# FFN-in: the lo parts of the weight operands and of the next pass's left operands computed on VectorE

## The chip, the cores and the metric

The kernel runs on one core of a Trainium2 chip. The metric is the device time of one execution in microseconds (us). Five engines work side by side, each through its own queue in order: TensorE (PE; its weight loads are PEld), VectorE (DVE), ScalarE (ACT), GpSimd (POOL), and SyncE (SP), which here only issues DMAs.

## The reference

One layer of a decoder over a prompt of 2048 tokens and 8 sample tokens, width 1024: norm, an input projection into a convolution group and a differential-attention group, an output projection, and a SwiGLU FFN of inner width 2816, all in float32. The change lies in the first half of the FFN:

```
h2 = rmsnorm(x, g_ffn) * (1 + sc_f) + sh_f
gg, uu = jnp.split(h2 @ w_ffn_in, 2, axis=-1)
x = x + gt_f * ((jax.nn.silu(gg) * uu) @ w_ffn_out)
```

## The kernel before

**Precision.** A float32 product is made of three TensorE products. Each operand is split into hi, a rounded copy (fp32r) that ScalarE casts, and lo, the operand minus hi, made by a subtraction on an engine that the caller names; then lo x hi, hi x lo and hi x hi are accumulated. The split is `split_sb` (lines 187 to 189): line 188 is the cast, line 189 the subtraction. Every lo part in the program carries line 189, so they are told apart by their tiles.

**FFN-in** (`phase_ffn_in`, lines 1097 to 1249) multiplies 2048 prompt rows and the 8 sample rows by w_ffn_in in three passes of 2 x 344 columns of h2 transposed (HW = 344, NPASS = 3). In a pass the product is a 2 x 2 block product done with seven block products instead of eight. The left operands of a pass are seven combinations a11, s1, s3, s2, a12, s4, a22 of the transposed rows, 128 x 1376 each, split into hi and lo tiles `cha..`/`cla..` and `chs..`/`cls..`; there is one buffer of each. A pass has 22 tiles of the inner width (f and f + 11 form a pair), 66 in all. `tile_f` (line 1149) does one tile:

- `w_combos` (line 1118) loads the two weight blocks of the tile (`wr`, four buffers), forms four block differences t1, t3, t2, t4 on VectorE (line 1128, tiles `tr`, four buffers), and splits the seven right operands b11, t1, t3, t2, b21, b22, t4, 128 x 512 each, into `wh`/`wl` tiles, one buffer for each operand. So an operand of the next tile can be split as soon as its block product of this tile is done, and must be there a tile later. Before, t1 and t4 have their lo part on VectorE and the other five on GpSimd (lines 1136 to 1146).
- seven block products of 12 matmuls each (line 1161), into PSUM tiles `in` (six buffers, four a tile);
- ScalarE copies one result (line 1167) and applies silu (lines 1175, 1180); VectorE adds the others from PSUM (line 1164, five a tile) and multiplies by silu (line 1181).

After each pair, `pair` (line 1184) makes the gating sums that the next phase's block product needs, four operations of 128 x 344 on GpSimd (lines 1193 to 1196), and SyncE stores them to gD (line 1200). The loads of the weight blocks (line 123, `ld`) go through the same SyncE queue.

During a pass, `next_raws` (line 1202) prepares the next pass: it loads rows, transposes them on TensorE (line 899, eight at a time), and forms the sums s1, s3, s2, s4 (line 907; s2 on GpSimd, the others on VectorE). At the end of the pass (lines 1245 to 1247) the seven new left operands are split; before, those with i % 3 == 2, s3 and s4, on GpSimd, the others on VectorE. The left operands of pass 0 are made by `first_combos` and by lines 1113 to 1116, which the change leaves as they are: a22 has its lo part on GpSimd there.

**Order.** Nothing in the kernel fixes the order across tiles. The program is traced in the order of the code, and the framework (`schedule_with_timeline_sim=True`, line 1534) lays out each engine's queue at build, by the dependences, the buffers and a simulated timeline. So an operation of the next tile stands between those of this one where the timeline found room. On the chip every queue runs in the order laid out.

Of the kernel before, what the change touches and what calls it, by code (L numbers as in the profile page):

```python
# [82 lines left out]
class Kern:  # L83
# [1013 lines left out]
    def phase_ffn_in(self, raws, comb):  # L1097
# [12 lines left out]
        dv, gp = nc.vector, nc.gpsimd  # L1110
        split = lambda *x: self.block_split(wp, *x)
# [6 lines left out]
        def w_combos(f):  # L1118

            raw = []  # L1120
            for part in range(2):
                r = self.t(wp, [P, KD, P], F32, "wr", bufs=4)
                c0 = part * DFF + f * P
                self.ld(r, I["w_ffn_in"][0, :, c0:c0 + P].rearrange("(k p) n -> p k n", p=P))
                raw.append(r.rearrange("p k n -> p (k n)"))
            b11, b21, b12, b22 = (raw[i][:, 512 * q:512 * (q + 1)] for i in range(2) for q in range(2))
            t1, t3, t2, t4 = (self.t(wp, [P, 512], F32, "tr", bufs=4) for _ in range(4))
            sub = lambda o, x, y: dv.tensor_tensor(out=o, in0=x, in1=y, op=ALU.subtract)
            out = {}

            def wsplit(i, name, r, eng):
                hi, lo = (self.t(wp, [P, 512], F32R, f"w{x}{i}") for x in "hl")
                self.split_sb(hi, lo, r, eng)
                out[name] = tuple(t.rearrange("p (k n) -> p k n", k=4) for t in (hi, lo))

            wsplit(0, "b11", b11, gp)
            sub(t1, b12, b11)
            wsplit(1, "t1", t1, dv)
            sub(t3, b22, b12)
            wsplit(2, "t3", t3, gp)  # L1140
            sub(t2, b22, t1)
            wsplit(3, "t2", t2, gp)
            wsplit(4, "b21", b21, gp)
            wsplit(5, "b22", b22, gp)
            sub(t4, b21, t2)
            wsplit(6, "t4", t4, dv)
            return out

        def tile_f(f, p, g):


            w = w_combos(f)
            t = self.t(wp, [P, 3, HW], F32, "nat", bufs=2)
            s, u2, u4 = (t[:, i] for i in range(3))
# [29 lines left out]
        def pair(f, p, work):  # L1184

            x = self.t(wp, [P, 3, HW], F32, "xt", bufs=3)
            y = self.t(wp, [P, 3, HW], F32, "xt", bufs=3)
            tile_f(f, p, x)
            work()
            t = tile_f(f + NF // 2, p, y)  # L1190
            work()
            cs = slice(HW * p, HW * (p + 1))
            gp.tensor_tensor(out=x[:, 2], in0=x[:, 1], in1=y[:, 1], op=ALU.add)
            gp.tensor_tensor(out=y[:, 2], in0=x[:, 2], in1=x[:, 0], op=ALU.subtract)
            gp.tensor_tensor(out=x[:, 1], in0=x[:, 0], in1=x[:, 1], op=ALU.subtract)
            gp.tensor_tensor(out=t[:, 0], in0=y[:, 0], in1=y[:, 2], op=ALU.subtract)

            st = nc.scalar if (f, p) == (NF // 2 - 1, NPASS - 1) else nc.sync
            for i, src in ((0, x), (3, y), (6, t[:, 0:1])):
                st.dma_start(out=self.gD[f][:, i:i + src.shape[1], cs], in_=src)  # L1200

        def next_raws(p):

            raws = self.new_raws()
            lo, w = half_pos(p)
            hi = lo + 2 * w

            pst = lambda: self.t(self.ps, [P, 512], F32, "tp", bufs=2)
            if w < HW:
                ht = self.t(wp, [DEC, D], F32, "gt")  # L1210
                self.ld(ht, self.h2sD)
                for q in range(2):
                    dv.memset(raws[1, q][:, :, w:], 0.0)
                    pt = pst().rearrange("p (k t) -> p k t", k=4)
                    for k in range(4):
                        nc.tensor.transpose(pt[:, k, 0:DEC], ht[:, (4 * q + k) * P:(4 * q + k + 1) * P], self.ident[:DEC, :DEC])
                    nc.scalar.copy(out=raws[0, q][:, :, w:], in_=pt[:, :, 0:DEC])
            for tt in range(lo // P, -(-hi // P)):
                self.turn_x1(raws, p, tt, "gt" if tt % 2 else "A2", pst)
                yield  # L1220
            s1, s2, s4 = (self.t(wp, [P, 4, HW], F32, f"rw{x}") for x in ("s1", "s2", "s4"))
            self.block_sum(s1, raws[1, 0], raws[1, 1], ALU.add, dv)
            yield
            self.block_sum(raws[1, 0], raws[0, 0], raws[1, 0], ALU.subtract, dv)
            self.block_sum(s2, s1, raws[0, 0], ALU.subtract, gp)
            yield
            self.block_sum(s4, raws[0, 1], s2, ALU.subtract, dv)
            yield {"a11": raws[0, 0], "s1": s1, "s3": raws[1, 0], "s2": s2, "a12": raws[0, 1], "s4": s4, "a22": raws[1, 1]}

        for p in range(NPASS):  # L1230
            ahead = next_raws(p + 1) if p + 1 < NPASS else iter(())
            nxt, done = None, 0

            def work():
                nonlocal nxt, done
                done += 1
                if (p, done) == (0, 4):
                    self.roots(6, 11)
                    self.roots(11, NT)
                if done > 6:  # L1240
                    nxt = next(ahead, nxt)

            for f in range(NF // 2):
                pair(f, p, work)
            if nxt:
                for i, (name, raw) in enumerate(nxt.items()):
                    comb[name] = split(name, raw, gp if i % 3 == 2 else dv)
        self.close("l3")
        self.close("r4")

# [287 lines left out]
```

## Time and profile before

| | |
|---|---|
| runs shown | median 2721.44 us of 3 (2715.95 to 2722.97) |
| profiled execution | 2719.35 us, its span 2717.6 us |
| TensorE clock granted, mean | 0.978 |
| HBM read and written | 283.10 MB, 106.12 MB |
| HBM traffic | 143 GB/s over the span |

Times are us from the start of the span, durations of one instruction ns where marked so. "Busy" counts the time from an instruction's start to its end, also when it is held up inside. "<-" behind a wait names what ended it. In the FFN-in stage the first matmul starts at 1297.0 and the last ends at 2234.7. The stretches used below begin and end where a tile's 84 matmuls do: at the starts of every 84th matmul of line 1161.

### The profile page before, as it was taken

How to read it: one execution, taken by the hardware profiler on the slowest of the kernel's cores; microseconds unless marked ns; L12 is line 12 of the kernel's file. 1: busy time of each engine (PE TensorE's matmuls, PEld its weight loads, DVE VectorE, ACT ScalarE, POOL GpSimd, SP SyncE). 2: the span in 40 equal slices, each digit the busy share in tenths (PEclk: the TensorE clock that was granted, in tenths of full speed). 3: DMA queues.
4: the chain of work that ended last, by engine and by line, in shares of the span. 5: the costliest groups of instructions: out<-in, count | busy, mean ns of one | idle time of the engine just before them, and what ended most of it. 6: DMA issues, size and time to landing. Idle time of an engine off the chain costs nothing.

```text
span 2717.6 us, 38141 instructions
## 1 busy us (share of the span) xinstructions
PE 2563.3 (94%) x13470; PEld 2154.6 (79%) x13470; DVE 1913.7 (70%) x2905; ACT 1250.5 (46%) x2385; POOL 1268.9 (47%) x902
## 2 busy tenths in 40 slices
PE   8999999998799998999799999999999989999997
PEld 3466767776687866777799999999899987778875
DVE  3269889987997887776767777776867653455467
ACT  4434222127797875473445343544434434333333
POOL 0100134024632223332667777667877753465573
PEclk9999999998999998999899999999999999999998
DMA  8635224238433314343344434434344435767555
GB/s 275 210 114 195 94 105 140 98 144 246 147 97 114 94 44 146 120 142 106 104 130 130 133 107 133 152 105 134 99 133 123 132 119 185 254 209 228 158 175 183
DMA packets 343991, 391.24 MB, mean 144 GB/s; under 512 B 31828, under 2 KB 258271, under 8 KB 343793
## 3 DMA queue, kind: packets, MB, share of 16 engines
q1 hardware_dynamic: 335945, 370.80, 42.6%
q10 hardware_dynamic: 7856, 18.01, 1.9%
q8 instruction: 106, 1.74, 0.3%
q14 instruction: 84, 0.69, 0.1%
HBM read 283.10 MB, written 106.12 MB: 143 GB/s over the span
## 4 chain that ended last, share of the span: by engine, by line
PE 51%; DVE 10%; issue 8%; POOL 5%; DMA 2%; ACT 2%; SPq 0%; ACTq 0%; POOLq 0%; DVEq 0%
PE in L1161 26%; PE o L1341 8%; PE one L155 2%; PE one L156 2%; PE one L154 2%; DVE p L660 2%; POOL wl L189 1%; PE two L655 1%; PE two L656 1%; PE x L844 1%; POOL w L1273 1%; POOL z L1273 1%; PE x L154 1%; DVE p L675 1%; PE x L156 1%
## 5 line engine op out<-in xcount | busy, mean ns | idle before, releaser
L1341 PE MATMUL o<-b,a 128*128 128x512 f32 x1848 | 431.8, 395 | 13.9 <-POOL b L189 11.4
L1341 PEld LDWEIGHTS o<-b,a 128*128 128x128 f32 x1848 | 348.0, 188 | 97.1 <-POOL b L189 12.2
L1161 PE MATMUL in<-cls,wh 128*128 128x344 f32 x1056 | 335.6, 324 | 27.3 <-DVE nat L1164 10.3
L1161 PE MATMUL in<-chs,wl 128*128 128x344 f32 x1056 | 341.5, 323 | 8.0 <-DVE wl L189 8.0
L189 POOL TENSOR_TENSOR wl<-wr,wh 128x512 fp32r<-128x512 f32 x198 | 296.2, 1504 | 107.3 <-ACT wh L188 105.9
L1161 PE MATMUL in<-chs,wh 128*128 128x344 f32 x1056 | 339.3, 321 | 0.0
L477 DVE SCALAR_TENSOR_TENSOR y<-u,cw,y 128x1024 f32<-128x1024 f32 x240 | 307.8, 1305 | 2.1
L188 ACT CAST wh<-tr 128x512 fp32r<-128x512 f32 x264 | 162.7, 620 | 207.0 <-PE in L1161 180.9
L1161 PE MATMUL in<-cla,wh 128*128 128x344 f32 x792 | 256.5, 324 | 1.2 <-ACT wh L188 0.7
L1161 PE MATMUL in<-cha,wl 128*128 128x344 f32 x792 | 254.9, 322 | 0.0
L1161 PE MATMUL in<-cha,wh 128*128 128x344 f32 x792 | 252.5, 321 | 0.0
L189 POOL TENSOR_TENSOR wl<-tr,wh 128x512 fp32r<-128x512 f32 x132 | 200.3, 1521 | 86.0 <-ACT wh L188 82.2
L672 POOL TENSOR_TENSOR p<-p,p 128x384 f32<-128x384 f32 (+9 forms) x60 | 109.0, 1819 | 251.6 <-ACT p L671 204.2
L498 POOL TENSOR_TENSOR ropet<-ev,tab 128x128 f32<-128x128 f32 x32 | 21.4, 670 | 433.5 <-ACT ev L531 433.1
L1161 PEld LDWEIGHTS in<-cls,wh 128*128 128x128 f32 x1056 | 199.0, 190 | 30.8 <-DVE nat L1164 10.8
L1161 PEld LDWEIGHTS in<-chs,wl 128*128 128x128 f32 x1056 | 200.6, 190 | 9.1 <-DVE wl L189 9.1
L1161 PEld LDWEIGHTS in<-chs,wh 128*128 128x128 f32 x1056 | 201.0, 190 | 0.0
L189 POOL TENSOR_TENSOR b<-wr,b 128x512 fp32r<-128x512 f32 x77 | 125.6, 1648 | 155.1 <-ACT b L188 155.0
L189 DVE TENSOR_TENSOR a<-gr,a 128x1032 fp32r<-128x1032 f32 (+1 forms) x77 | 116.6, 1522 | 109.1 <-ACT a L188 109.0
L188 ACT CAST wh<-wr 128x512 fp32r<-128x512 f32 x198 | 122.5, 620 | 100.2 <-POOL wl L189 46.0
L664 ACT ACTIVATE p<-p,st 128x384 f32<-128x384 f32 (+15 forms) x128 | 156.4, 1224 | 20.2 <-DVE st L660 15.3
L154 PE MATMUL one<-w,hTh 128*128 128x512 f32 x384 | 154.4, 405 | 8.0 <-DVE w L189 4.8
(351 smaller groups left out, 6487.4 us busy)
## 6 DMA issues: line engine op xcount, KB each, us to landing
wr<-in_w_ffn_in SPq DMA_DIRECT2D x132, 512.0 KB
gD<-xt SPq DMA_DIRECT2D x64, 516.0 KB
wr<-in_w_ffn_out SPq DMA_DIRECT2D x99, 256.0 KB
gr<-gD SPq DMA_DIRECT2D x44, 516.0 KB
w<-in_w_in SPq DMA_DIRECT2D x80, 256.0 KB
gr<-gD SPq DMA_DIRECT2D x33, 512.0 KB
xt<-in_x_prompt SPq DMA_DIRECT2D x32, 512.0 KB
a<-in_w_ada SPq DMA_DIRECT2D x64, 256.0 KB
```

Source lines behind the costliest of these rows:

```text
L154: mm(ps, lhsT=wh, rhs=xl, start=start, stop=False)
L155: mm(ps, lhsT=wl, rhs=xh, start=False, stop=False)
L156: mm(ps, lhsT=wh, rhs=xh, start=False, stop=stop)
L188: self.nc.scalar.copy(out=hi, in_=raw)
L189: (eng or self.nc.gpsimd).tensor_tensor(out=lo, in0=raw, in1=hi.bitcast(F32), op=ALU.subtract)
L477: nc.vector.scalar_tensor_tensor(out=y, in0=u[:, j:j + HALF], scalar=self.cw[:, ct, j:j + 1], in1=y, op0=ALU.mult, op1=ALU.add)
L660: dv.tensor_tensor_reduce(out=pc[:, lo:hi], in0=sc[:, 0:w], in1=add, scale=1.0, scalar=m, op0=ALU.add, op1=ALU.min, accum_out=mo)
L664: nc.scalar.activation(pc[:, 0:L], pc[:, 0:L], AF.Exp, bias=m, scale=-1.0, accum_out=l)
L672: nc.gpsimd.tensor_tensor(out=a, in0=a, in1=b, op=ALU.add)
L1161: nc.tensor.matmul(ps, lhsT=wt[:, k, :], rhs=xt[:, k, :], start=not more and k == 0 and j == 0, stop=k == 3 and j == 2, skip_group_check=True)
L1273: op = lambda e, o, x, y, k: e.tensor_tensor(out=o, in0=x, in1=y, op=k)
L1341: mm = lambda x, y, s, e: nc.tensor.matmul(ps[i], lhsT=a[:, x, sl], rhs=b[:, y], start=s, stop=e, skip_group_check=True)
```

## The change

Two edits in `phase_ffn_in`. The five lo parts of a tile that were on GpSimd (b11, t3, t2, b21, b22) are on VectorE, so that all seven are; and the lo parts of all seven left operands of the next pass are on VectorE. The casts, the products, the additions, the gating sums and the buffers are as before.

```diff
-            wsplit(0, "b11", b11, gp)
+            wsplit(0, "b11", b11, dv)
             sub(t1, b12, b11)
             wsplit(1, "t1", t1, dv)
             sub(t3, b22, b12)
-            wsplit(2, "t3", t3, gp)
+            wsplit(2, "t3", t3, dv)
             sub(t2, b22, t1)
-            wsplit(3, "t2", t2, gp)
-            wsplit(4, "b21", b21, gp)
-            wsplit(5, "b22", b22, gp)
+            wsplit(3, "t2", t2, dv)
+            wsplit(4, "b21", b21, dv)
+            wsplit(5, "b22", b22, dv)
             sub(t4, b21, t2)
             wsplit(6, "t4", t4, dv)
...
             if nxt:
-                for i, (name, raw) in enumerate(nxt.items()):
-                    comb[name] = split(name, raw, gp if i % 3 == 2 else dv)
+                for name, raw in nxt.items():
+                    comb[name] = split(name, raw, dv)
```

## Rows read from the trace of the kernel before

**Rows 1.** The page, busy time, share of the span and instructions.
```profile
PE 2563.3 (94%) x13470; PEld 2154.6 (79%) x13470; DVE 1913.7 (70%) x2905; ACT 1250.5 (46%) x2385; POOL 1268.9 (47%) x902
```
**Rows 2.** Stretch, length, busy PE, PEld, DVE, ACT, POOL (instructions); clock, DMA share, GB/s.
```profile
1297.00:1329.35 32.35, 18.51 (x92) 17.75 (x93) 28.50 (x35) 15.10 (x28) 22.98 (x12) 0.74 0.27 82
...
1479.85:1510.87 31.02, 27.38 (x170) 26.40 (x169) 29.51 (x27) 12.63 (x23) 26.79 (x16) 1.00 0.36 112
1510.87:1603.51 92.64, 92.64 (x591) 92.64 (x590) 62.70 (x85) 38.09 (x70) 66.87 (x49) 1.00 0.41 128
1603.51:1651.75 48.24, 42.51 (x254) 41.16 (x253) 45.32 (x43) 23.09 (x38) 41.52 (x23) 0.96 0.32 98
...
1748.62:1828.04 79.42, 73.85 (x446) 72.98 (x445) 61.34 (x64) 39.92 (x86) 53.42 (x36) 0.94 0.35 110
...
1920.68:1968.78 48.10, 42.53 (x254) 41.17 (x253) 45.66 (x41) 23.19 (x38) 42.14 (x23) 0.96 0.33 99
```
**Rows 3.** The chain, 1400 to 1430: start, length, what; one set of transposes.
```profile
1418.35 0.88 PE tp L899 x8
```
**Rows 4.** Timeline of VectorE in ordinary tiles: start, duration, operation.
```profile
2107.05 1.42 DVE L189 TENSOR_TENSOR wl<-tr,wh 128x512 fp32r<-128x512 f32 x1
2109.14 1.03 DVE L1128 TENSOR_TENSOR tr<-wr,wr 128x512 f32<-128x512 f32 x1 [0.67 <-DMA wr<-in_w_ffn_in]
...
2119.21 0.86 DVE L1181 TENSOR_TENSOR xt<-xt,dm 128x688 f32<-128x688 f32 x1
2119.99 0.68 DVE L1128 TENSOR_TENSOR tr<-wr,tr 128x512 f32<-128x512 f32 x1
2120.60 0.68 DVE L189 TENSOR_TENSOR wl<-tr,wh 128x512 fp32r<-128x512 f32 x1
```
**Rows 5.** Timeline of GpSimd, the same tiles.
```profile
2106.61 1.31 POOL L1193 TENSOR_TENSOR xt<-xt,xt 128x344 f32<-128x344 f32 x1 [2.12 <-DVE xt L1181]
2107.89 1.74 POOL L189 TENSOR_TENSOR wl<-tr,wh 128x512 fp32r<-128x512 f32 x1
```
**Rows 6.** Groups of VectorE in the stage: count, busy us, mean ns, idle before.
```profile
L1164 DVE TENSOR_TENSOR xt<-in,nat 128x344 f32<-128x344 f32 x132 | 68.0, 515 | 70.0 <-PE in L1161 67.9
```
**Rows 7.** Line 189, whole span: count, duration ns min/median/max, first and last start.
```profile
L189 POOL TENSOR_TENSOR wl<-wr,wh x198: 1275/1301/2661, 1305.1 to 2223.5; 128x512 fp32r<-128x512 f32 x198
...
L189 DVE TENSOR_TENSOR wl<-tr,wh x132: 676/925/3653, 1314.6 to 2224.7; 128x512 fp32r<-128x512 f32 x132
...
L189 DVE TENSOR_TENSOR cls<-rws,chs x4: 1580/1906/2235, 1611.0 to 1935.2; 128x1376 fp32r<-128x1376 f32 x4
L189 POOL TENSOR_TENSOR cls<-rws,chs x3: 3614/3616/4248, 1209.5 to 1941.2; 128x1376 fp32r<-128x1376 f32 x3
```
**Rows 8.** Line 1196 in the stage, one of the four gating sums.
```profile
L1196 POOL TENSOR_TENSOR nat<-xt x32: 914/932/1385, 1354.9 to 2219.5; 128x344 f32<-128x344 f32 x32
```
**Rows 9.** Waits of SyncE's queue in the stage: us in total, times, longest.
```profile
SPq L123 <- POOL wl L189: 434.8, 126, 10.5
```
**Rows 10.** Waits of VectorE in the stage.
```profile
DVE xt L1164 <- PE in L1161: 67.9, 52, 4.7
DVE tr L1128 <- DMA wr<-in_w_ffn_in: 46.0, 37, 2.5
DVE B L1164 <- PE in L1161: 42.7, 31, 1.4
DVE dm L1164 <- PE in L1161: 32.3, 25, 1.4
```
**Rows 11.** Timeline of VectorE at the entry.
```profile
1302.12 3.58 DVE L1128 TENSOR_TENSOR tr<-wr,wr 128x512 f32<-128x512 f32 x1
...
1314.62 0.68 DVE L189 TENSOR_TENSOR wl<-tr,wh 128x512 fp32r<-128x512 f32 x1
```
**Rows 12.** Timeline of GpSimd at the entry.
```profile
1300.71 4.44 POOL L189 TENSOR_TENSOR cla<-rw,cha 128x1376 fp32r<-128x1376 f32 x1
```

## The prediction

> **What bounds the kernel now.** I began with the busy shares of the page [rows 1]: over the whole span VectorE (DVE) is at 70% and GpSimd (POOL) at 47%, so by shares there is room on GpSimd and less on VectorE, and the change moves work the wrong way. An average over stages says little, so next I cut the FFN-in stage at the starts of tiles and took busy time by stretch [rows 2]. A tile here is one call of tile_f, 84 matmuls; there are 66. The stretch from 1510.87 to 1603.51 holds seven tiles and TensorE is busy for all of its 92.64 us, so a tile costs 92.64 / 7 = 13.23 us when nothing is late. There TensorE is the only bound, and a faster VectorE or GpSimd gains nothing. What can be won or lost is in the other stretches, each against 13.23 us a tile:
> - the entry, one tile in 32.35: 19.1 us lost;
> - the block sums of the pass that follows, two tiles in 31.02: 4.6 us lost;
> - the change from pass 0 to pass 1, three tiles in 48.24: 8.5 us lost;
> - the transposes and block sums late in pass 1: five tiles in 79.42, which is 13.3 over; four sets of eight transposes at 0.88 us each [rows 3] are TensorE's own work, so 9.7 us lost;
> - the change from pass 1 to pass 2, three tiles in 48.10: 8.4 us lost.
>
> That is 50 us, 1.8% of the time, and no part of the change reaches another stage. The next view says why those stretches are late. In the order of time on VectorE [rows 4] a 512-column subtraction takes 0.68 us and the next one starts 0.61 us later, but others take 1.42 and 1.03. Beside them stand GpSimd's rows [rows 5]: its instruction from 2106.61 ends at 2107.92, and the VectorE subtraction begun at 2107.05 ends at 2108.47, 0.55 us after that. GpSimd's next, from 2107.89 to 2109.63, takes 1.74 us instead of some 1.26, and the VectorE subtraction begun at 2109.14 ends 0.54 us after it. So an operation of GpSimd and one of VectorE with both inputs in SBUF do not overlap here: the later one waits, and the recorded duration holds the wait. The two engines are one resource for such work. Operations that read one input from PSUM don't show this: their mean is 0.52 us [rows 6].
>
> **That resource, per tile.** The shortest durations stand for work without a wait [rows 7]: 1.27 us for a 512-column lo part on GpSimd; 0.68 on VectorE, of which 0.61 counts in a row. Before: on VectorE six 512-column operations (2 lo parts, 4 block differences) at 0.61 and one product at 0.78 (2119.21 to 2119.99, [rows 4]), 4.4 us; on GpSimd five lo parts at 1.27 and two gating sums (four per pair of tiles) at 0.91 [rows 8], 8.2 us. Together 12.6 of 13.23 us, 95% taken. In an ordinary tile that just fits; where anything is added, it doesn't, and TensorE waits.
>
> **The change, part by part.**
> 1. Five lo parts a tile leave GpSimd (330 in all): 5 x 1.27 = 6.4 us a tile given back. On VectorE they come as 5 x 0.61 = 3.1 us. The resource falls to 12.6 - 6.4 + 3.1 = 9.3 us, 70%.
> 2. VectorE's own queue: eleven operations at 0.61, five additions from PSUM at about 0.5, the product at 0.78: 10.0 us a tile. To that come waits for the gating sums that stay on GpSimd, between none and all of them, 0 to 1.8 us: 10.0 to 11.8 of 13.23. Before, it is busy 62.70 / 7 = 8.96 us a tile [rows 2], of which 7.0 is its own work by the same prices (six operations, five additions, the product) and 2.0 is waiting for GpSimd. So the ordinary tile costs nothing: its 3.1 us more lie beside TensorE's 13.23. If that cover went, every 0.1 us a tile would cost 66 x 0.1 = 6.6 us.
> 3. At each of the two pass changes the lo parts of s3 and s4 (1376 columns) move too: two times 3.61 us off GpSimd, two times 1.58 onto VectorE [rows 7].
> 4. The waits that move. The next tiles' weight loads in SP's queue wait for the last reader of a raw block, until now a GpSimd lo part for 126 of them [rows 9], and the stores of the gating results stand in the same queue. Now VectorE releases the blocks; a lo part there takes half as long but stands behind additions that wait for TensorE. VectorE already waits 46.0 us in 37 places for these loads [rows 10], with lo parts queued behind. An earlier release saves at most those 46 us of slack, and a later one adds to them; a lo part is needed about six products (six sevenths of 13.23, some 11 us) after its slot comes free, so I take 0 for both and keep the effect for the slower rival. ScalarE's casts into the same slots then wait for VectorE instead of GpSimd; same reason, 0.
>
> **The sum, by stretch.** The loss is less than the excess over TensorE's time, because slots give some slack: in the first pass change the resource needed 3 x 12.6 + 5 x 1.58 + 2 x 3.61 = 52.9 us for tiles of 39.7 in all, an excess of 13.2 for a loss of 8.5, so about 4.7 us is forgiven.
> - Pass changes: afterwards VectorE's queue is the longer of the two: 3 x (10.0 to 11.8) + 7 x 1.58 = 41.1 to 46.5 us, an excess of 1.4 to 6.8; less 4.7, a loss of 0 to 2.1. Since an in-order queue also waits, I take 3.5 left of 8.5: 5 us saved at each, ends 0 and 8.5.
> - Block sums of pass 0: the resource needed 2 x 12.6 + 3 x 1.58 + 3.61 (the sum s2 on GpSimd, by the lo part of its shape) = 33.6 for 26.5; VectorE afterwards 2 x 10.0 + 4.7 plus up to 3.6 of waiting for s2 and up to 3.6 for the gating sums: 24.7 to 32. Saved 0 to 4.6, taken 2.
> - Pass 1's late stretch has the same sums and besides transposes fed by loads: saved 0 to 6, taken 2.
> - The entry: the first difference of weight blocks takes 3.58 us instead of 0.68, behind a GpSimd split of 4.44 us that the change leaves there [rows 12], and t1's lo part comes only at 1314.62 [rows 11]. The lo parts that leave GpSimd free a few waits of about 1 us, and come into the same VectorE queue ahead of t1. Ends 3 lost and 8 saved, taken 2.
>
> Saved: 5 + 5 + 2 + 2 + 2 = 16 us. The profiled execution took 2719.35 us (span 2717.6), so 2703 against it; it lies 2 us under the median of the runs, 2721.44, and I give the median's side: 2705.
>
> **Against a rule.** VectorE's busy time in the ordinary stretch is 62.70 of 92.64 us, 68% [rows 2]. The Trainium skill, Perfetto Trace Analysis, section Identifying the Most-Contended Engine, takes the occupancy of VectorE as a fair measure of how near it is to its limit, and its section on Optimizing Scalar/DVE Operations would hand work from a saturated VectorE to other engines, GpSimd included. By that, 8.96 + 3.1 = 12.0 us a tile, 91%, and any stretch with more work saturates; the rows speak against it, since 2.0 of the 8.96 is waiting that goes.
>
> **The rivals.**
> A. *No change that can be measured.* A measurement of this kernel tells about 0.3%, 8 us, from nothing. The order of each engine's instructions is laid down at build from estimated times, and in it VectorE's heads wait for TensorE and for loads; then the stretches are late for that order, not for GpSimd. Saved 1 to 2 us at each pass change and nothing else: about 2718. For it: the first wait of the entry isn't touched. Against: the excess of 13.2 us at a pass change is mostly GpSimd's durations.
> B. *VectorE's in-order queue becomes the bound of the ordinary tile.* Its additions already wait for TensorE 67.9 + 42.7 + 32.3 = 142.9 us in the stage [rows 10], 2.2 a tile. If those waits stay where they are and the gating sums are waited for in full, 11.8 + 2.2 = 14.0 us is over 13.23. It decides once both waits together pass 3.2 us a tile. Halfway, at 0.4 us over on 60 tiles, 24 us are lost, less some 10 recovered: 2721 + 14 = 2735; at the full 0.8, near 2757. This is the case that the rule above describes. Against: a queue that is late finds TensorE's results ready, so such waits shrink first.
> C. *The change does more.* All of the loss at the pass changes and most at the sums goes: 8.5 + 8.4 + 4.6 + 6 + 4 = 31 us, 2690. This is the far end of the forecast, not a case of its own sign.
>
> **How the numbers follow.** Forecast (faster by 8 us or more, C included) 0.60, A 0.26, B 0.14. The likeliest time is 2705; its own range runs from 2690 to 2713. To leave out no more than 2 in 10 the range must hold A with the spread of the runs, to 2723, and the near end of B: 2690 to 2728.
>
> **What would show it.** Right: in the ordinary stretches of seven tiles still 92.6 us with GpSimd's busy time down from 66.87 to some 13 to 19 us and VectorE's up from 62.70 to between 70 and 83; VectorE's 512-column lo parts close to 0.68 us at the median; three tiles of a pass change in 43 to 44 us. Wrong: ordinary tiles longer than 13.3 us with TensorE waiting for VectorE's lo parts (B); pass changes still near 48 us with VectorE idle in them (A); an entry longer than 35 us; or VectorE operations still near 1 us while GpSimd is idle, which would mean that the wait wasn't GpSimd's.

## The result, and the profile after

The changed kernel takes 2683.11 us (median of 4 runs, 2680.43 to 2686.02) against 2721.03 us for the kernel before: a ratio of 0.9856, interval 0.984 to 0.9872. It is faster by 38 us; 2705 was predicted, with 2690 as the lower end of the range. The profiled execution took 2683.30 us, its span is 2681.5. Ratios, here and below, are of fast runs; two slow executions, 14162.85 us of the kernel before and 9932.47 us of the last kernel below, are not in them.

The first part of the page, busy time over the whole span, to hold beside [rows 1]:

```profile
PE 2553.9 (95%) x13470; PEld 2148.5 (80%) x13470; DVE 2000.0 (75%) x3239; ACT 1257.0 (47%) x2385; POOL 763.7 (28%) x568
```

VectorE has 334 instructions more and GpSimd 334 fewer. GpSimd gave up 505 us of busy time, and VectorE took on only 86 us for the same work. 330 lo parts at 0.61 us alone are 201 us, so over 100 us of what VectorE had recorded as busy before was waiting.

The next rows are stretches of the stage in the changed kernel, cut at the starts of the same tiles as in [rows 2] (stretch, length, busy PE, PEld, DVE, ACT, POOL with instructions; clock, DMA share, GB/s): the entry, the block sums of pass 0, seven ordinary tiles, the first pass change, the late stretch of pass 1, the second pass change.

```profile
1299.14:1324.14 25.00, 16.70 (x97) 16.39 (x98) 24.96 (x40) 15.80 (x32) 7.96 (x2) 0.80 0.41 127
1473.75:1500.61 26.86, 26.76 (x169) 26.43 (x169) 25.79 (x34) 11.73 (x21) 9.41 (x5) 1.00 0.40 124
1500.61:1593.31 92.70, 92.70 (x591) 92.70 (x589) 80.07 (x121) 38.99 (x70) 20.30 (x16) 1.00 0.43 133
1593.31:1636.14 42.83, 42.83 (x278) 42.11 (x277) 41.96 (x62) 30.53 (x58) 5.28 (x4) 1.00 0.46 141
...
1729.93:1799.13 69.20, 69.20 (x446) 68.72 (x445) 59.27 (x86) 38.89 (x85) 15.25 (x9) 1.00 0.40 121
...
1891.85:1932.01 40.16, 39.96 (x255) 39.70 (x253) 40.16 (x56) 22.22 (x35) 5.86 (x4) 1.00 0.38 110
```

In all but the entry PE's busy time fills the length to within 0.2 us: TensorE is now the bound there, as it was before in the ordinary tiles alone. VectorE has little left in the second pass change: it is busy for all of the 40.16 us. Row by row against [rows 2]:

| stretch | before | after | difference | predicted |
|---|---|---|---|---|
| entry, 1 tile | 32.35 | 25.00 | -7.35 | -2 |
| block sums of pass 0, 2 tiles | 31.02 | 26.86 | -4.2 | -2 |
| ordinary, 7 tiles | 92.64 | 92.70 | 0 | 0 |
| first pass change, 3 tiles, and the 7 after it | 145.11 | 136.62 | -8.5 | -5 |
| late in pass 1, 5 tiles | 79.42 | 69.20 | -10.2 | -2 |
| second pass change, 3 tiles | 48.10 | 40.16 | -7.9 | -5 |
| the other 38 tiles | 508.96 | 507.32 | -1.6 | 0 |

The first pass change stands with the seven tiles behind it, since 24 transposes moved from those into it (278 instructions on PE instead of 254). The stage as a whole goes from 937.7 to 897.8 us. It starts 2.1 us later and what follows it takes 1.7 us longer, which leaves the 36.1 us by which the span is shorter. Over TensorE's pace of 13.23 us a tile, and some 0.11 us for each of the stage's 104 transposes, it lost some 52.6 us before and 12.7 after, and 10.4 of those 12.7 are in the entry.

Not all of the gain is waiting that went away. These are the sums over the stage's stretches (length, busy time of each engine), before and after:

```profile
sum 937.60, PE 901.86 PEld 895.14 DVE 682.10 ACT 416.03 POOL 677.69; mean PE 90.19 PEld 89.51 DVE 68.21 ACT 41.60 POOL 67.77
```

```profile
sum 897.86, PE 889.24 PEld 886.48 DVE 766.33 ACT 422.42 POOL 174.55; mean PE 88.92 PEld 88.65 DVE 76.63 ACT 42.24 POOL 17.46
```

TensorE stands still for 35.7 us before (937.60 - 901.86) and for 8.6 after, 27.1 us less. The other 12.6 us are time in which it works, though its instructions are the same. Most of that, some 10 us, is its clock. In the rows of the two pass changes and of the late stretch of pass 1 it was granted at 0.96, 0.96 and 0.94 before [rows 2], and at 1.00 after; (1 - clock) x length is 8.6 us there, and outside the entry TensorE's busy time fell by 10.8. At the entry the clock was 0.74 and is 0.80, a difference of some 2 us of work. The first pass change before shows it (TensorE, start and duration):

```profile
1636.91 0.40 PE L1161 MATMUL in<-cls,wh 128*128 128x344 f32 x1 [4.03 <-POOL xt L1193]
...
1638.00 0.49 PE L1161 MATMUL in<-chs,wh 128*128 128x344 f32 x1
1638.29 0.49 PE L1161 MATMUL in<-cls,wh 128*128 128x344 f32 x1
```

TensorE had stood still for 4.03 us, and soon after it its matmuls start 0.29 us apart, at the lower level of its clock (1.2 GHz), instead of 13.23 / 84 = 0.16. So a wait costs its own length and slower work behind it, and the prediction has no term for the second.

VectorE's waits in the stage (us in total, times, longest), to hold beside [rows 10]:

```profile
DVE tr L1128 <- DMA wr<-in_w_ffn_in: 46.8, 41, 3.3
...
DVE xt L1164 <- PE in L1161: 19.1, 15, 2.8
DVE B L1164 <- PE in L1161: 11.0, 19, 1.4
DVE dm L1164 <- PE in L1161: 9.9, 20, 0.6
```

The additions wait 40.0 us for TensorE, where it was 142.9. The wait for loads did not move: 46.0 before, 46.8 now.

Line 189 in the stage (count, duration min/median/max in ns, first and last start), to hold beside [rows 7]:

```profile
L189 DVE TENSOR_TENSOR wl<-tr,wh x264: 672/685/1459, 1312.4 to 2186.9; 128x512 fp32r<-128x512 f32 x132
...
L189 DVE TENSOR_TENSOR wl<-wr,wh x198: 651/681/3577, 1304.2 to 2185.0; 128x512 fp32r<-128x512 f32 x198
...
L189 DVE TENSOR_TENSOR cls<-rws,chs x6: 1582/1582/1593, 1596.6 to 1912.9; 128x1376 fp32r<-128x1376 f32 x6
```

The median lo part is at its own 0.68 us, where it was 0.93, and six 1376-column ones lie between 1.582 and 1.593 us where four had a median of 1.906.

GpSimd's last gating sum of each pair, with the same columns, to hold beside [rows 8]:

```profile
L1196 POOL TENSOR_TENSOR nat<-xt x32: 1367/1381/1396, 1349.1 to 2179.6; 128x344 f32<-128x344 f32 x32
```

Its median is 1.38 us where it was 0.93: it now takes turns with VectorE's lo parts, and nobody is late for it.

What TensorE itself waits for in the stage, before:

```profile
PE in L1161 <- DVE nat L1164: 10.3, 10, 2.9
PE in L1161 <- ACT wh L188: 9.7, 2, 8.9
PE in L1161 <- POOL xt L1193: 8.1, 2, 4.0
PE in L1161 <- DVE wl L189: 8.0, 4, 4.9
```

and after, where nothing else is over 0.2 us:

```profile
PE in L1161 <- DVE wl L189: 8.3, 1, 8.3
PE in L1161 <- ACT wh L188: 0.7, 1, 0.7
```

No row of the kernel before names a lo part of GpSimd; TensorE's weight loads name one in one place, for 0.2 us. The two waits of 4.0 us, one at each pass change, are put down to a gating sum of GpSimd (line 1193), of whose result TensorE reads nothing. At the first pass change that sum ended at 1636.77, and in the same moment, at 1636.76, two additions of VectorE from TensorE's accumulators; the matmul waited for VectorE as well:

```profile
1635.74 1.02 DVE L1164 TENSOR_TENSOR nat<-in,nat 128x344 f32<-128x344 f32 x2
```

The wait of 8.9 us is at the entry, for the cast of t1, whose block difference is the one that takes 3.58 us [rows 11]. So these waits lead to VectorE's queue.

What held that queue can be seen in two timelines of VectorE (start, duration, operation). First the kernel before, in the first pass change:

```profile
1624.65 3.65 DVE L1128 TENSOR_TENSOR tr<-wr,tr 128x512 f32<-128x512 f32 x1
1628.22 0.50 DVE L1164 TENSOR_TENSOR xt<-in,nat 128x344 f32<-128x344 f32 x1
1628.64 0.50 DVE L1164 TENSOR_TENSOR B<-in,nat 128x344 f32<-128x344 f32 x1
```

and GpSimd beside it:

```profile
1624.13 3.61 POOL L189 TENSOR_TENSOR cls<-rws,chs 128x1376 fp32r<-128x1376 f32 x1
1627.70 1.74 POOL L189 TENSOR_TENSOR wl<-wr,wh 128x512 fp32r<-128x512 f32 x1
```

The subtraction begun at 1624.65 needs 0.68 us and is done at 1628.30, 0.56 us after GpSimd's 1376-column lo part has ended at 1627.74. Everything behind it in VectorE's queue is 3 us late, the additions that free TensorE's accumulators among it. Now the changed kernel, the same place in the pass:

```profile
1600.74 0.68 DVE L1128 TENSOR_TENSOR tr<-wr,tr 128x512 f32<-128x512 f32 x1
1601.35 1.58 DVE L189 TENSOR_TENSOR cls<-rw,chs 128x1376 fp32r<-128x1376 f32 x1
1602.85 0.51 DVE L1164 TENSOR_TENSOR nat<-in,nat 128x344 f32<-128x344 f32 x1
```

The 1376-column lo part is now VectorE's own, and it costs 1.58 us instead of a wait of 3.

### The profile page after: what moved, and what is told of

Read it like the earlier page. It is cut to its first block, busy times and chain, and to the rows that moved or that the text cites. A ratio compares the mean times of both kernels' runs of the same rounds, so it can differ in the third digit from the quotient of the medians.

```text
span 2681.5 us, 37944 instructions
## 1 busy us (share of the span) xinstructions
PE 2553.9 (95%) x13470; PEld 2148.5 (80%) x13470; DVE 2000.0 (75%) x3239; ACT 1257.0 (47%) x2385; POOL 763.7 (28%) x568
## 4 chain that ended last, share of the span: by engine, by line
issue 31%; PE 27%; POOL 8%; DVE 8%; DMA 2%; ACT 1%; SPq 1%; POOLq 0%; ACTq 0%; DVEq 0%
PE o L1341 10%; PE one L155 3%; PE one L156 2%; PE one L154 2%; DVE p L660 2%; POOL nat L1196 2%; POOL xt L1193 1%; PE two L655 1%; POOL xt L1194 1%; PE two L656 1%; PE x L844 1%; POOL w L1273 1%; POOL z L1273 1%; PE x L154 1%; DVE al L185 1%
## 5 line engine op out<-in xcount | busy, mean ns | idle before, releaser
L1341 PE MATMUL o<-b,a 128*128 128x512 f32 x1848 | 432.8, 396 | 13.8 <-POOL b L189 11.4
L1193 POOL TENSOR_TENSOR xt<-xt,xt 128x344 f32<-128x344 f32 x33 | 39.2, 1187 | 687.2 <-DVE xt L1181 616.1
L189 DVE TENSOR_TENSOR wl<-tr,wh 128x512 fp32r<-128x512 f32 x264 | 211.1, 805 | 18.7 <-ACT wh L188 12.4
L1161 PEld LDWEIGHTS in<-cha,wl 128*128 128x128 f32 x792 | 149.4, 189 | 8.5 <-DVE wl L189 8.5
```

Source lines behind the costliest of these rows:

```text
L189: (eng or self.nc.gpsimd).tensor_tensor(out=lo, in0=raw, in1=hi.bitcast(F32), op=ALU.subtract)
L1161: nc.tensor.matmul(ps, lhsT=wt[:, k, :], rhs=xt[:, k, :], start=not more and k == 0 and j == 0, stop=k == 3 and j == 2, skip_group_check=True)
L1341: mm = lambda x, y, s, e: nc.tensor.matmul(ps[i], lhsT=a[:, x, sl], rhs=b[:, y], start=s, stop=e, skip_group_check=True)
```

## The experiments

Theory 1 is the prediction's: an operation of GpSimd and one of VectorE with both inputs in SBUF exclude each other, so GpSimd's lo parts cost VectorE time, and VectorE is what TensorE waits for. The main rival is that GpSimd was simply slow: 1.27 us where VectorE takes 0.68, so its lo parts came late, or what waits behind them did (slots, stores), and no exclusion is needed. Thirteen kernels tell these apart, and with them the parts of the change. Ratios are to the kernel before, on the same chip; its medians there were 2719.2 to 2723.06 us.

### One part alone: the weights

The change without its last edit, so that two lo parts of the next pass's left operands (1376 columns) stay on GpSimd at each pass change:

```diff
-            wsplit(0, "b11", b11, gp)
+            wsplit(0, "b11", b11, dv)
...
-            wsplit(5, "b22", b22, gp)
+            wsplit(5, "b22", b22, dv)
```

> Only the five lo parts of a tile move to VectorE; s3 and s4 of the next pass keep their lo part on GpSimd. Theory 1 (VectorE's operations with two SBUF inputs and GpSimd's exclude each other, and that was what made VectorE late): a pass change then needs 3 x 9.3 + 5 x 1.58 + 2 x 3.61 = 43 us of the shared resource for tiles of 39.7, which the slack of about 4.7 forgives: within 3 us of the changed kernel, 2683 to 2686. Theory 2 (GpSimd's own lo parts came too late for TensorE, with no effect on VectorE's operations): also near 2683, since two splits do not make GpSimd late. If the second edit carries a large part of the gain: 2690 or more.

2694.73 us, ratio 0.9888 (0.9867 to 0.991): 26 us won, 12 fewer than the whole change. The profiled stage takes 908.6 us, 10.8 more than with the whole change; what follows it takes 6.7 more and what precedes it 4.1 less, where the edit has no part. Its two pass changes (columns as above):

```profile
1590.22:1635.84 45.62, 42.27 (x266) 40.66 (x265) 44.12 (x58) 23.70 (x42) 13.05 (x6) 1.00 0.36 109
1893.31:1938.57 45.26, 42.29 (x254) 41.11 (x253) 44.50 (x57) 23.70 (x38) 12.78 (x6) 0.96 0.33 97
```

By tiles they lose 4.3 and 5.6 us, and the cause stands in the second one's timelines, VectorE's first and GpSimd's behind it:

```profile
1902.10 3.24 DVE L189 TENSOR_TENSOR wl<-tr,wh 128x512 fp32r<-128x512 f32 x1
...
1910.92 4.25 DVE L189 TENSOR_TENSOR wl<-wr,wh 128x512 fp32r<-128x512 f32 x2
```

```profile
1901.22 3.58 POOL L189 TENSOR_TENSOR cls<-rw,chs 128x1376 fp32r<-128x1376 f32 x1 [10.35 <-ACT chs L188]
1910.05 3.98 POOL L189 TENSOR_TENSOR cls<-rws,chs 128x1376 fp32r<-128x1376 f32 x1 [5.26 <-ACT chs L188]
```

Two long operations of GpSimd in 45 us suffice to make TensorE late, now that VectorE's queue holds everything else. My sum of a shared resource had room for them, so the scale was wrong. VectorE's own queue, with each GpSimd operation waited for once, gives 3 x (10.0 to 11.8) + 5 x 1.58 + 2 x 3.6 = 45.1 to 50.5 us; less 39.7 of TensorE and the 4.7 forgiven, 0.7 to 6.1 lost. That holds 4.3 and 5.6.

### The other part alone: the left operands

```diff
-                    comb[name] = split(name, raw, gp if i % 3 == 2 else dv)
+                    comb[name] = split(name, raw, dv)
```

> Only the lo parts of the next pass's left operands move. Theory 1: a pass change needs 3 x 12.6 + 7 x 1.58 = 48.9 us of the shared resource instead of 52.9, so each of the two loses 4 us less: 2713, and no other stretch changes. Theory 2: GpSimd keeps 5 lo parts a tile and loses two of 3.6 us at each pass change, so its results are about 4 to 7 us earlier there: 2707 to 2713. If the order laid out anew is what helps, any value from 2683 to 2721.

2716.4 us, ratio 0.9977 (0.9961 to 0.9994): 4.5 us. In the profiled stages the two parts nearly add up, 29.1 + 7.0 = 36.1 of 39.9 us. This kernel's late pass 1 loses 4.7 us instead of 10.6 (79.42 less five tiles and the 24 transposes in it), though the edit touches nothing there. So part of a stretch's loss goes with how the order falls out, and a single stretch can be read to a few us only.

### GpSimd work that nobody needs

The cleanest cut between the theories. All lo parts are on VectorE as in the changed kernel, and GpSimd gets five subtractions a tile of the hi part from itself, whose result nothing reads, once of 256 columns and once of 512, as many as the change took away (n is 256 or 512; the lines are set out for reading):

```diff
             self.split_sb(hi, lo, r, eng)
+            if i not in (1, 6):
+                h, gx = hi[:, 0:n].bitcast(F32), self.t(wp, [P, 512], F32, "gx")[:, 0:n]
+                gp.tensor_tensor(out=gx, in0=h, in1=h, op=ALU.subtract)
```

> The changed kernel with five unneeded GpSimd subtractions of 256 columns a tile, into a scratch tile that nobody reads; nothing waits for their result. Theory 1: the shared resource goes from 9.3 to 9.3 + 5 x 0.69 = 12.7 us of 13.23 a tile, as full as in the kernel before: most of the gain is lost again, 2705 to 2725, and VectorE's 512-column operations show means near 1 us instead of 0.7 to 0.9. Theory 2: nobody waits for GpSimd, so 2683 to 2687 and VectorE's durations as in the changed kernel.

> The same with 512 columns, the full load that the change took off GpSimd. Theory 1: 9.3 + 5 x 1.27 = 15.6 us of the shared resource for 13.23 of TensorE, so the ordinary tile itself becomes longer: up to 66 x 2.4 = 158 us, 2760 to 2840, slower than the kernel before. Theory 2: 2683 to 2690.

With 256 columns 2698.69 us (0.9901, 0.9878 to 0.9924), 16 more than the changed kernel and less than I expected. With 512 columns 2819.45 us, ratio 1.0343 (1.0316 to 1.0371): 136 us more than the changed kernel, and slower than the kernel before. Two stretches of the second, its lo parts and the unneeded work itself:

```profile
1500.00:1600.00 100.00, 89.40 (x550) 87.34 (x549) 92.09 (x111) 34.32 (x65) 64.72 (x47) 0.98 0.34 106
1650.00:1750.00 100.00, 88.20 (x533) 84.16 (x533) 95.47 (x116) 42.33 (x83) 56.66 (x43) 0.98 0.38 117
```

```profile
L189 DVE TENSOR_TENSOR wl<-tr,wh x241: 672/1097/1561, 1314.6 to 2239.4; 128x512 fp32r<-128x512 f32 x121
```

```profile
L1134 POOL TENSOR_TENSOR gx<-wh x330: 1035/1371/3198, 1306.9 to 2323.9; 128x512 f32<-128x512 f32 x165
```

VectorE's operations are the same as in the changed kernel, yet they fill 92 and 95 of 100 us. The median lo part of a block difference takes 1.10 us instead of 0.69; that of a raw block stays at 0.68, so not every one meets GpSimd. GpSimd's own median is 1.37 against a shortest of 1.04. Both pay. TensorE gets nothing from GpSimd that it didn't get in the changed kernel, and is busy for 88 to 89 of 100 us. What it and ScalarE wait for:

```profile
ACT nat L1167 <- DMA gD<-nat: 109.1, 28, 7.4
...
PE in L1161 <- DVE nat L1164: 62.2, 53, 2.5
```

TensorE waits for VectorE's additions, as theory 1 has it. But the first row is a second path. The last gating sum is written into t, the "nat" buffer that ScalarE's copy of the next tiles needs again, so late gating sums make late stores, and these hold ScalarE and with it TensorE. That path belongs to the rival, and it had to be priced.

### The same with the store's path taken away

The last gating sum gets a tile of its own, so that ScalarE's copy never waits for its store:

```diff
+            t = self.t(wp, [P, 1, HW], F32, "g6")
             gp.tensor_tensor(out=t[:, 0], in0=y[:, 0], in1=y[:, 2], op=ALU.subtract)
```

First in the kernel before, with nothing else:

> The kernel before with the last gating sum in a tile of its own, and nothing else; the order of VectorE's and TensorE's instructions stays. ScalarE waited 74.1 us there for the stores, and 36.2 in the changed kernel. If a part of the change's gain came by that way (earlier gating sums, earlier stores, earlier casts): faster than before, 2700 to 2715. If the gain came from VectorE's waits for GpSimd alone: 2717 to 2723.

2720.56 us, ratio 1.0006 (0.9993 to 1.0019): nothing. In the kernel before this path carried no time that the change could have won. The order of VectorE and TensorE is the same in both kernels, and yet the entry loses 14.8 us here and 18.2 there (without the eight transposes that it holds in both), the block sums 6.7 and 4.6: so much one stretch moves between executions. Then in the two kernels with unneeded work:

> The changed kernel with the five unneeded GpSimd subtractions of 512 columns, and the last gating sum in a tile of its own, so that nothing of ScalarE waits for the stores of GpSimd's late gating sums. If the 136 us that these subtractions cost come from VectorE's waits for GpSimd: 2780 to 2820, and VectorE stays over 90% busy in the ordinary tiles. If they came from the store chain (ScalarE waited 91.1 us there against 36.2): 2683 to 2720.

> The same with 256 columns. If VectorE's waits made the loss of 16 us: 2692 to 2702. If the store chain made it (79.3 us of waits against 36.2): 2681 to 2687.

2785.27 us (1.0229, 1.0207 to 1.0251) and 2692.24 us (0.9883, 0.9865 to 0.9901). Of 136 us 102 remain, of 16 us 9. Three quarters of the larger cost thus come without that store. Its waits:

```profile
PE in L1161 <- DVE nat L1164: 58.1, 53, 4.3
ACT B L1180 <- DVE B L1164: 56.7, 27, 5.2
```

What TensorE and ScalarE wait for is VectorE, and VectorE itself waits for no store and nothing of GpSimd among its waits in the stage, while the lo parts of block differences still take 1.10 us at the median, and those of raw blocks 0.97. One way past VectorE is left: the unneeded subtractions read the hi tiles, of which there is one each, so ScalarE's next cast can wait for them. With 512 columns it did so for 1.5 us in 2 places, with 256 for 24.8 in 20. The 102 us are hardly touched by that; the 9 us are no clean price of VectorE's waits. Theory 1 stands; "GpSimd was slow" falls as the main cause, here and by TensorE's waits in the kernel before, of which 0.2 us in all ended with a lo part of GpSimd. (The order of VectorE's instructions isn't wholly that of the changed kernel: 119 of 3239 of them stand elsewhere in the 512-column kernel, 77 in the one with the own tile. And the own tile was not tried in the changed kernel alone.)

### GpSimd's other work

If exclusion is all, then taking the four gating sums off GpSimd should help the kernel before too, in which GpSimd keeps five lo parts a tile:

```diff
-            gp.tensor_tensor(out=x[:, 2], in0=x[:, 1], in1=y[:, 1], op=ALU.add)
+            dv.tensor_tensor(out=x[:, 2], in0=x[:, 1], in1=y[:, 1], op=ALU.add)
...
-            gp.tensor_tensor(out=t[:, 0], in0=y[:, 0], in1=y[:, 2], op=ALU.subtract)
+            dv.tensor_tensor(out=t[:, 0], in0=y[:, 0], in1=y[:, 2], op=ALU.subtract)
```

> The kernel before with the four gating sums of a pair on VectorE instead, and the lo parts left as they were. Theory 1: per tile 1.8 us of GpSimd's holding become 0.9 us of VectorE's, 12.6 to 11.7 of the shared resource; the pass changes need 2.8 us less and the block sums 1.9, so 7 to 10 us saved: about 2712, far less than what the five lo parts gave, because these hold the resource 6.4 us a tile. If what counts is only that some work leaves GpSimd: 2690 or less.

2757.72 us, ratio 1.0146 (1.0129 to 1.0163): 37 us slower, where 2712 was expected. The shared resource is emptier in this kernel (four operations of 0.9 us became four of about 0.5), and it is slower. VectorE between two GpSimd lo parts, in one pair of tiles:

```profile
1350.32 0.51 DVE L1193 TENSOR_TENSOR xt<-xt,xt 128x344 f32<-128x344 f32 x1
1350.94 1.59 DVE L1128 TENSOR_TENSOR tr<-wr,wr 128x512 f32<-128x512 f32 x1
1352.45 1.60 DVE L1194 TENSOR_TENSOR xt<-xt 128x344 f32<-128x344 f32 x1
1353.98 0.50 DVE L1195 TENSOR_TENSOR xt<-xt 128x344 f32<-128x344 f32 x1
...
1354.83 1.53 DVE L1128 TENSOR_TENSOR tr<-wr 128x512 f32<-128x512 f32 x1
1356.29 1.60 DVE L1196 TENSOR_TENSOR nat<-xt 128x344 f32<-128x344 f32 x1
```

Those that meet a GpSimd lo part take 1.53 to 1.60 us, those that don't 0.50. The mean of lines 1193 to 1195 is 1.2 us: that is what a gating sum costs in VectorE's queue, more than on GpSimd. The same edit on the changed kernel, where GpSimd has next to nothing left in the stage, and the same on the kernel before with the store's path taken away:

> The changed kernel with the gating sums on VectorE too, so that GpSimd does nothing in an ordinary tile. Theory 1: VectorE's 11.4 us a tile (80.07 us busy in seven tiles) lose their waits for GpSimd, about 1.4, and gain 0.9 of own work: a little less than 11.4, under TensorE's 13.23 either way, so no change but for the entry and the pass changes, 2680 to 2686. If VectorE's queue is already at its limit: slower, 2690 or more.

> The slow kernel with the gating sums on VectorE, with one thing more: the last gating sum goes into a tile of its own, so that ScalarE's copy of a later tile no longer waits for its store. Theory A (the store chain made it slow: ScalarE waited 94.7 us for those stores, with casts queued behind): those waits go and most of the 37 us with them, 2720 to 2735. Theory B (VectorE's additional two-input operations stand between GpSimd's lo parts and wait for each): the chain is a side effect, 2745 to 2760.

2680.49 us (0.9847, 0.9833 to 0.9861), the same as the changed kernel; and 2736.5 us (1.0075, 1.0056 to 1.0094). Against the kernel before on the same chip it was 37 us slower and is now 17, so some 20 came through the store, and 17 remain, which theory 1 lays to VectorE's longer queue. The cost of moving an operation onto VectorE depends on what GpSimd still does beside it.

### What is left at the entry, and the rest of GpSimd's lo parts

The split of the left operand a22, 4.44 us on GpSimd at the entry [rows 12], was left there by the change:

```diff
-        comb["a22"] = split("a22", raws[1, 1], gp)
+        comb["a22"] = split("a22", raws[1, 1], dv)
```

> The changed kernel with the first a22's lo part (1376 columns) on VectorE too, instead of GpSimd. At the entry the first lo part of b11 is held 3.58 us instead of 0.68 by that GpSimd operation of 4.44 us. Theory 1 (mutual exclusion): 2.9 us of waiting go and 1.58 us of VectorE's own come, and the next operations no longer wait: the entry's loss of 10 us shrinks by 1 to 4 us, 2679 to 2682. If the entry is bound by the chain of the output projection and the weight blocks instead, no change, 2683; if the longer queue of VectorE decides, 2684 to 2685.

2681.66 us (0.9859, 0.9844 to 0.9874), the same as the changed kernel. TensorE's one long wait at the entry goes from 8.3 to 6.9 us and the tile's loss from 10.4 to 9.9. The split that GpSimd kept was not what holds the entry, then. Of the 10.4 us, 8.3 are one wait, for the first lo part of b11, and some 2 are slower work behind it, at the clock of 0.80. In the kernel with a22 on VectorE that wait runs beside VectorE's own queue, which has no gap there: two lo parts of left operands (5.22 us from 1291.47, with GpSimd's addition of the output projection, 3.56 us, beside them), a block sum (1.58), and then the one waited for, at 1298.12. Whether another order there would help was not tried. Two versions that move more, this one with the lo parts of FFN-out's b (line 1330) on VectorE, and one with a22, the gating sums and the block sum s2 (line 1225) there:

> As with a22 on VectorE, and in FFN-out the 77 lo parts of the weight operands moved from GpSimd to VectorE. There TensorE waits 11.4 us for GpSimd's lo parts, of which 9.6 at its start, where the gating sums and the stores come first. Theory 1: VectorE is busy about half of that stage, so the move is free, and 1 to 5 us are won on top of the a22 edit: 2675 to 2681. If VectorE's additions from PSUM there are pushed back: 2683 to 2690.

> Everything of the stage but the output projection's additions on VectorE: the changed kernel with a22's first lo part, the gating sums and the sum s2 moved too. VectorE's own work is some 10.9 us a tile with nothing to wait for: ordinary tiles stay at TensorE's 13.23, and only the entry (10 us lost) and odds of 1 us elsewhere can gain: 2674 to 2683. If VectorE's queue becomes the bound at the pass changes: 2685 to 2695.

2678.24 us (0.9851, 0.9832 to 0.9871) and 2680.97 us (0.9858, 0.9833 to 0.9883). Neither beats the changed kernel by more than the spread, and FFN-out's first wait for a lo part is 9.1 us on VectorE where it was 9.6. TensorE is the bound in this stage now, and moving more off GpSimd has nothing to win.

## Why the prediction was wrong in size

The direction, the mechanism and the place were as predicted; the size was 38 us instead of 16. Two terms of the sum by stretch failed: the 3.5 us that were left standing at each pass change, where 0.4 and 0.5 remained, and TensorE's slower clock behind its waits, which stood in no term and gave back some 10 us. Step by step:

- **What bounds the stage.** Ordinary tiles cost nothing before and after, 92.64 and 92.70 us. All but 1.6 us of the gain lies in the stretches that were named.
- **Exclusion.** Held, by the median of the lo parts (0.93 to 0.68 us) and above all by work that nobody needs, at 102 us with the store's path taken away.
- **VectorE's own queue.** 10.0 to 11.8 us a tile was the sum; 80.07 / 7 = 11.4 was measured, near the top. GpSimd's 20.30 us lie just above the 13 to 19 named as right, since the gating sums now take turns with VectorE's lo parts. VectorE is busy for 86% of the ordinary stretch and TensorE waits for nothing there. The Trainium skill, Perfetto Trace Analysis, section Identifying the Most-Contended Engine, would read such an occupancy as an engine near its limit, and by the sum of before it would have been 91%; the measurement decides against that reading here. The Trainium skill, Perfetto Trace Analysis, section Optimizing Scalar/DVE Operations, which the prediction cites for handing work to GpSimd, goes on that the two engines share an SBUF read port, so that moving work between them might not help. The prediction doesn't weigh that; these runs agree, since work moved off GpSimd cost VectorE's busy time 86 us and freed GpSimd's by 505. A busy time that holds waits is no fixed quantity to add to.
- **Weight loads and slots, taken at 0.** Held: 46.0 and 46.8 us of waits. SP now waits 504.0 us in 121 places for VectorE's lo parts, where it waited 434.8 for GpSimd's [rows 9], and it costs nothing.
- **The sum by stretch: here it failed.** "Since an in-order queue also waits, I take 3.5 left of 8.5" was a reserve that no row bore out. My own working gave 0 to 2.1 left at a pass change, and 0.4 and 0.5 are left. The argument that stood under rival B, that a queue which is late finds TensorE's results ready and one that is early waits harmlessly, was the one that came true (142.9 to 40.0 us of waits), and I used it against B but not for the forecast. The block sums were put at 2 of 0 to 4.6 and gave 4.2. The entry was put at 2 of -3 to 8 and gave 7.4. Late in pass 1 even the bound was too small: 0 to 6 was set, and the stretch gave back 10.2. It had 10.6 to lose and not 9.7, since three sets of transposes stand in it and not four. Of the 10.2, 5.6 are TensorE's waits (79.42 - 73.85 before, nothing after), within the bound; the other 4.6 are TensorE's busy time, 73.85 against 69.20 for the same 446 instructions, at a clock of 0.94 and 1.00.
- **The clock, in no term.** Losses were read against 13.23 us a tile, so they held TensorE's slower work, but the sum priced queues and waits alone. By the sums over the stage 27.1 us of the gain are waits and 12.6 are working time, of which the clock is some 10.
- **Choosing the low side each time.** Five terms, each taken below what the working itself gave as the middle, added up to 16. (The pass changes were taken at 5 of ends of 0 and 8.5, but the working left only 0 to 2.1 standing.) The middles would have been 7.4 at each pass change (8.5 less half of 2.1), 2.3 and 3 at the sums and 2.5 at the entry: 22.6 us, or some 2699. The far end, case C at 31 us and 2690, was still 7 us short, most of it in pass 1 and at the entry.
- **One resource that is added up.** This picture gave the right direction and the wrong numbers, in the weights alone (2683 to 2686 expected, 2694.73 measured), in the unneeded 256 columns and in the gating sums (2712 expected, 2757.72 measured). The queue that serves TensorE, with one wait for each GpSimd operation that it meets, came nearer in the weights alone, where it was worked out.
- **The rivals.** A (order, not GpSimd) forecast about 2718 and falls as the whole cause, by the time and by the unneeded work; B did not come about.

What stays open: the change also lays out the order anew (145 of the 2905 instructions that VectorE has in both stand elsewhere), and how much of the 38 us belongs to that was not separated. The own-tile kernel kept the order and gained nothing, which says nothing of another order. Nor was anything tried that shortens the entry, 10 us late still.

## What to carry to other kernels

Before adding up busy times of VectorE and GpSimd, compare the median of each kind of instruction with its shortest: the difference can be waiting for the other engine, and here it went away with that engine's work. When TensorE waits, look at the clock granted to it behind the wait: here some 10 of the stage's 40 us were slower work and not waiting. Where VectorE serves TensorE in order, give the elementwise work with two SBUF inputs to one of the two engines, the long operations first, since two of 3.6 us left on GpSimd cost 4 to 6 us in a stretch; moving the short half onto VectorE while the long half stays on GpSimd can make it slower. When the sum of a queue says that a loss disappears, take that as the forecast and keep the reserve for the range.

## What the runs showed of the hardware

A subtraction of one kind that GpSimd does beside VectorE costs both: with the unneeded work of 512 columns 1.37 us at the median against a shortest of 1.04 on GpSimd, and 1.10 against 0.67 on VectorE for the lo parts of block differences.

I had not expected that a tiny operation with a single SBUF tensor as its input is held too. At the entry of the kernel before, VectorE, with GpSimd at work from 1300.71 to beyond 1311 without a gap:

```profile
1307.30 1.25 DVE L139 TENSOR_SCALAR rsq<-rx 128x5 f32<-128x5 f32 x1
...
1310.23 0.16 DVE L141 TENSOR_SCALAR rsq<-rsq 128x5 int32<-128x5 int32 x1
```

and after, where GpSimd had ended at 1307.26:

```profile
1309.53 0.16 DVE L139 TENSOR_SCALAR rsq<-rx 128x5 f32<-128x5 f32 x1
```

Five elements a partition, 1.25 us and 0.16. The additions with one input from PSUM took 0.50 us beside a GpSimd operation too: those of 1628.22 and 1628.64 in the timeline of the kernel before lie within GpSimd's lo part of 1627.70 to 1629.44. The Trainium skill, SBUF — State Buffer, section Who interferes with whom, says that VectorE and GpSimd share one pair of ports under an exclusive lock, that a VectorE operation takes it for a second SBUF input, and that tensor_scalar can take it in its modes with two ports, whereas one SBUF input beside PSUM does not. The rows agree on all three: 3.65 against 0.68, 1.25 against 0.16, and 0.50 unchanged. The third tensor_scalar, on int32, took 0.16 us, but it began at 1310.23, where one operation of GpSimd ended and the next began; whether it needs no lock or slipped in between, no run here tells.
